# Weighted sums over keys in three 64-column passes, in a hybrid SSD and attention layer

## The chip, the cores and the metric

The kernel runs on one NeuronCore of a Trainium2 chip. The metric is the device time of one execution in microseconds (us). Five engines work side by side, each on its own queue in order: PE (TensorE, the matrix multiplier; PEld is its weight loader), DVE (VectorE), ACT (ScalarE), POOL (GpSimd) and SP (SyncE, which here issues the DMAs). PE writes its results to PSUM, of which the kernel uses 8 banks of 128 partitions by 512 columns; DVE and ACT read them back.

## The reference, cut to what matters

One decoder layer over 512 positions of width 1024: an RMS norm, then two mixers side by side (a Mamba-2 SSD with 16 heads of 64 and an attention with 16 heads of 64), an output projection, and a squared-ReLU MLP. All is float32. What the change touches is one step in each mixer, where a matrix of weights over keys multiplies the values of one head:

```python
# SSD, per head: y = (C B^T * decay, lower triangle) @ (dt * x), and then the skip
y = ssd_chunked_scan(xs, dt, a, bm, cm) + d_skip.astype(jnp.float32)[:, None] * xs
# attention, per head: softmax weights (three dilated windows joined) @ v
o = jnp.einsum('brhiqk,brhikd->brhiqd', pr, vb.astype(jnp.float32)) / denom
```

Both are, for one head, a 512 x 512 lower triangular matrix of weights W (queries by keys) times a 512 x 64 matrix of values t.

## The kernel before

**Split operands.** The kernel multiplies operands of type fp32r. It splits each float32 operand in two parts, hi (a cast to fp32r) and lo (what the cast left over, also cast), and adds up products of parts in PSUM. A dense product (`mm3`, lines 151 to 154) takes three passes: hi by hi, hi by lo, lo by hi.

**The weighted sum.** `weighted_sum` (lines 635 to 641) is called by `ssd_sum` and `att_sum`, once for each of 32 heads. W lies transposed, keys on partitions, in four blocks of 128 keys; block j holds only the queries that may see it: 512, 384, 256 and 128 of them (`BLK`), 1280 columns in all (`OFF` are their starts). There is a tile for its hi part (`wk_H`, `Wh` in the function) and one for its lo part (`wk_L`, `Wl`). The values of a pair of heads lie in one tile (`xd` for SSD, `vhl` for attention): for each block of keys and each head 64 columns of hi beside 64 columns of lo. The function loads these 128 columns as weights, so that rows 0 to 63 of the result hold (value hi) x W and rows 64 to 127 hold (value lo) x W, and passes W's hi part and W's lo part through them: 8 matmuls. All four products of parts are made. The two halves of the PSUM bank must then be added.

**Reading the result.** In SSD `ssd_add` (lines 707 to 713) does it on DVE: line 711 adds the skip to rows 0 to 63, line 713 adds rows 64 to 127. In attention `att_copy` (line 936) copies rows 0 to 63 on ACT to `ya`, and `att_add` (line 941) adds rows 64 to 127 on DVE. The bank is free after that last addition.

**What sets the order.** From 157 us to 507 us of the span the order on every engine is made by a planner, `place_units` (lines 1051 to 1119). The program states several hundred units of work, each with engine, cost in ns, what it needs and makes, what it takes from and gives back to pools of buffers, and a due time; a unit marked "ACT/DVE" or "POOL/DVE" has two costs and goes where it would end first. Again and again the planner takes, among the units that are ready, the one that can start first by these costs (with a slack, within which the earlier due time wins), and appends it to its engine's queue. In this stretch PE does five kinds of work: dense products of the input projection (`hh`, `hl`; 32 jobs of 24 matmuls) and of half of the output projection (`yh`, `yl`), which are due late and so fill gaps; score products (lines 866 and 869); transposes by a product with the identity (lines 649, 838, 912); sums over rows and spreads of scales (1218, 1219, 799, 732); and the 32 weighted sums (line 640). DVE does for each SSD head the product with the decay (line 693) and the lo part (701), for each attention head the row maxima (879), most normalisations (902) and the lo part (925), and beside them the dot products of the conditioning vector (280). The chip's engines then follow the queues in order, and wait at a semaphore where something that a unit needs is late.

Behind 507 us come the other half of the output projection and the MLP, which the change leaves as they were.

Of the kernel before, what the change touches and what calls it, by code (L numbers as in the profile page):

```python
# [17 lines left out]
P = 128  # L18
# [8 lines left out]
BLK = [512, 384, 256, 128]  # L27
# [17 lines left out]
def tile_hybrid_layer(ctx, tc, xT, vec, c_row, ada_e, ada_r, w_a, w_dt, w_x, w_z, w_v, w_qk,  # L45
# [588 lines left out]

    def weighted_sum(p, t, e, Wh, Wl):

        W = Wh, Wl
        for n, (j, i) in enumerate(((0, 0), (0, 1), (1, 0), (1, 1), (2, 0), (3, 0), (2, 1), (3, 1))):
            m = (2 * j + e) * P
            nc.tensor.matmul(p[:, j * P:], lhsT=t[:, m:m + P], rhs=W[i][:, OFF[j]:OFF[j] + BLK[j]],  # L640
                             start=n == 0, stop=n == 7)

    S = {}

# [58 lines left out]
    def ssd_sum(h, p):  # L703
        sums_o[h] = p
        weighted_sum(p, xdt[h // 2], h % 2, S.pop(("H", h)), S.pop(("L", h)))

    def ssd_add(h):
        c, e = h // 2, h % 2
        p = sums_o.pop(h)
        r = slice(e * 64, e * 64 + 64)  # L710
        nc.vector.scalar_tensor_tensor(xs[c][r], xs[c][r], vecs[r, V_DS + c:V_DS + c + 1], p[:64],
                                       op0=OP.mult, op1=OP.add)
        nc.vector.tensor_add(xs[c][r], xs[c][r], p[64:])

    def gate_mul(g):

# [215 lines left out]
    def att_copy(h):  # L932
        if h % 2 == 0:
            yatt.append(zp.tile([P, T], F32, tag="z8", name="ya"))
        r = slice(h % 2 * 64, h % 2 * 64 + 64)
        nc.scalar.copy(yatt[h // 2][r], S["ao", h][:64])

    def att_add(h):
        r = slice(h % 2 * 64, h % 2 * 64 + 64)
        y = yatt[h // 2]  # L940
        nc.vector.tensor_add(y[r], y[r], S.pop(("ao", h))[64:])

    def ssq_sq(pair):
        if pair:
# [101 lines left out]
    def unit(eng, cost, fn, needs=(), makes=None, take=(), give=(), due=0.0, lands=0):  # L1046
        units.append((eng, cost, fn, tuple(needs), makes, tuple(take), tuple(give), due, lands))
# [76 lines left out]
    def xbank(key):  # L1124
        return bank(2 + rooms["x", key])
# [139 lines left out]
    for h in range(16):  # L1265
        c = h // 2
        unit("SP", 350, lambda h=h: dec_load(h), [], ("A", h), [("A", ("s", h))], due=h - 2, lands=4500)
        unit("POOL", 1450, lambda h=h: dec_trim(h), [("A", h)], ("trim", h), due=h - 0.5)
        unit("ACT", 2150, lambda h=h: dec_exp(h), [("trim", h)] + ([] if h else [("z", 1)]), ("exp", h), due=h)
        needs = [("exp", h)] + ([("cb3", n) for n in range(3)] if h >= 12 else [("cb0", h // 4)])  # L1270
        unit("DVE", 1850, lambda h=h: wt_mul(h), needs, ("mul", h),
             give=[("cb", h // 4)] if h % 4 == 3 else [], due=h + 0.3)
        unit("ACT", 1270, lambda h=h: wt_hi(h), [("mul", h)], ("hi", h), [("H", ("s", h))], due=h + 0.4)
        unit("DVE", 2050, lambda h=h: wt_lo(h), [("hi", h)], ("lo", h), [("L", ("s", h))],
             [("A", ("s", h))], due=h + 0.5)
        unit("PE", 1180, lambda h=h: ssd_sum(h, xbank(("so", h))), [("hi", h), ("lo", h), ("xdt", c)],
             ("so", h), [("x", ("so", h))],
             [("H", ("s", h)), ("L", ("s", h))] + ([("xd", c)] if h % 2 else []), due=h + 0.6)
        unit("DVE", 1460, lambda h=h: ssd_add(h), [("so", h)], ("sy", h), give=[("x", ("so", h))],
             due=h + 0.8)  # L1280


# [94 lines left out]
    for a in range(16):  # L1377
        p, e = a // 2, a % 2
        t = AT + a
        A = ("A", ("a", a))  # L1380
        for n in range(3):
            k = ("sp", a, n)
            unit("PE", (440, 480, 260)[n], lambda a=a, n=n: att_scores(a, n, xbank(("sp", a, n))),
                 [("sk", p), ("sq", p), ("ql", p, e)] + ([("sp", a, n - 1)] if n else []), k, [("x", k)],
                 ([("ql%d" % e, p)] + ([("st", p)] if e else [])) if n == 2 else [], due=t)
            unit("DVE", (690, 850, 420)[n], lambda a=a, n=n: att_max(a, n),
                 [k, "mask"] + ([("mx", a, n - 1)] if n else []), ("mx", a, n), [A] if n == 0 else [],
                 [("x", k)], due=t + 0.1)
        unit("DVE", 180, lambda a=a: att_neg(a), [("mx", a, 2)], ("neg", a), due=t + 0.2)
        unit("ACT", 3050, lambda a=a: soft(*S["soft", a]), [("neg", a)], ("soft", a), due=t + 0.2)  # L1390
        unit("DVE", 170, lambda a=a: att_inv(a), [("soft", a)], ("inv", a), due=t + 0.4)
        for i in range(4):
            unit("ACT/DVE", ((370, 320), (480, 430), (600, 540), (730, 650))[i],
                 lambda eng, a=a, i=i: att_norm(a, i, eng), [("inv", a)], ("norm", a, i), due=t + 0.4)
        for n in range(3):
            k = ("fl", a, n)
            unit("PE", (460, 460, 230)[n], lambda a=a, n=n: att_flip(a, n, xbank(("fl", a, n))),
                 [("norm", a, i) for i in ((0, 1, 2, 3), (1, 2, 3), (2, 3))[n]], k, [("x", k)],
                 [A] if n == 2 else [], due=t + 0.5)
            unit("ACT", (590, 590, 375)[n], lambda a=a, n=n: att_hi(a, n),  # L1400
                 [k] + ([("ah", a, n - 1)] if n else []), ("ah", a, n), [] if n else [("H", ("a", a))],
                 due=t + 0.6)
            unit("DVE", (690, 690, 430)[n], lambda a=a, n=n: att_lo(a, n),
                 [("ah", a, n)] + ([("al", a, n - 1)] if n else []), ("al", a, n),
                 [] if n else [("L", ("a", a))], [("x", k)], due=t + 0.7)
        k = ("ao", a)
        unit("PE", 1180, lambda a=a: att_sum(a, xbank(("ao", a))), [("al", a, n) for n in range(3)] + [("vl", p, e)], k,
             [("x", k)], [("H", ("a", a)), ("L", ("a", a))] + ([("vhl", p)] if e else []), due=t + 0.8)
        unit("ACT", 590, lambda a=a: att_copy(a), [k], ("yc", a), [] if e else [("z8", ("y", p))],
             due=t + 0.9)  # L1410
        unit("DVE", 690, lambda a=a: att_add(a), [("yc", a)], ("ya", a), give=[("x", k)], due=t + 1)
        if e:
            k = ("ss", p)
            if p:
                unit("ACT", 630, lambda p=p: ssq_sq(p), [("ya", a), ("ya", a - 1)], k, [("f2", k)],
                     due=t + 1)
                unit("POOL", 1400, lambda p=p: ssq_add(p), [k, ("ssq", p - 1)], ("ssq", p),
                     give=[("f2", k)], due=t + 1)
            else:
                unit("ACT", 630, lambda p=p: ssq_sq(p), [("ya", a), ("ya", a - 1)], ("ssq", 0), due=t + 1)  # L1420
# [214 lines left out]
```

## Time and profile before

| | |
|---|---|
| time, median of 3 executions | 914.64 us (911.78 to 915.18) |
| the profiled execution's own time | 912.53 us, of which the span of its instructions is 910.8 us |
| granted TensorE clock, mean | 0.983 of full speed |
| busy share of the span | PE 93%, DVE 69%, ACT 48%, POOL 30% |
| stretch made by the planner | 157 to 507 us, 350 us |
| in it: PE, DVE, ACT, POOL busy | 323.67, 308.85, 242.29, 210.35 us |

The views of a profile are these. The page gives busy times, the span in 40 slices, and the chain of work that ended last, followed back from the last instruction. The view of groups puts instructions of one line, engine and form in one row: busy time, mean duration, and the engine's idle time just before them. The view of windows gives each engine's busy time in a stretch. The view of waits says who waited for whom. The timeline lists instructions in order of start. Matmuls are pipelined and their ends are modelled: in a row of matmuls each starts before the one ahead has ended, and the time that each costs is the distance from start to start.

### The profile page before, as it was taken

To read this page: it belongs to the slowest core of one execution; us is meant where nothing else is said; L and a number is where in the kernel's file an instruction comes from. 1 tells how busy PE (TensorE), PEld (TensorE's weight loads), DVE (VectorE), ACT (ScalarE), POOL (GpSimd) and SP (SyncE) were. 2 spreads that over 40 slices of the span, in tenths; PEclk is the share of its full clock that TensorE was granted. 3 is DMA by queue.
4 is the path that set the end of the run, shared out by engine and by line. 5 is a ranking of instruction groups with operands and counts; after the bars stand their busy time and mean duration, and the time that the engine had idled before them with its cause. 6 is when DMAs were issued, how large, how long until landed. Compare 5 with 4: busy or idle time off the path is not lost.

```text
span 910.8 us, 11334 instructions
## 1 busy us (share of the span) xinstructions
PE 851.4 (93%) x4112; PEld 709.8 (78%) x4112; DVE 624.2 (69%) x1017; ACT 436.6 (48%) x759; POOL 277.7 (30%) x177
## 2 busy tenths in 40 slices
PE   4988899999898778999899998999999999999998
PEld 4656787878786667788787798988888888888887
DVE  7999976898999889986988678764322234343321
ACT  4225446769664467777866535343212233332110
POOL 3323336486978736556242212000000000000000
PEclk9999999999999999999999999999999999999999
DMA  9743345443644734433442323452232222333320
GB/s 330 255 161 121 109 130 194 156 157 128 212 136 137 230 99 141 129 102 116 140 139 70 116 59 127 152 195 93 96 111 94 93 93 94 106 101 104 119 100 24
DMA packets 43111, 120.01 MB, mean 132 GB/s; under 512 B 5264, under 2 KB 5792, under 8 KB 43056
## 3 DMA queue, kind: packets, MB, share of 16 engines
q1 hardware_dynamic: 43056, 119.29, 40.0%
q8 instruction: 32, 0.52, 0.2%
q14 instruction: 23, 0.19, 0.1%
HBM read 108.70 MB, written 2.18 MB: 122 GB/s over the span
## 4 chain that ended last, share of the span: by engine, by line
PE 65%; DVE 25%; DMA 3%; ACT 3%; issue 3%; POOL 0%; SPq 0%; DVEq 0%; POOLq 0%
PE ps L152 19%; PE ps L153 19%; PE ps L154 19%; PE ps L640 3%; DVE wa L280 3%; DVE ada L280 3%; DMA ada<-in_ada_r_dram 2%; DVE wk_L L701 2%; DVE wk_A L902 1%; DVE wk_A L879 1%; DVE wk_A L693 1%; DVE f L585 1%; ACT wk_A L85 1%; PE ps L912 1%; DVE raw L804 1%
## 5 line engine op out<-in xcount | busy, mean ns | idle before, releaser
L114 ACT CAST whi<-wraw 128x1024 fp32r<-128x1024 f32 (+1 forms) x84 | 86.4, 1031 | 247.7 <-PE ps L153 225.1
L117 DVE TENSOR_TENSOR wlo<-wraw,whi 128x1024 fp32r<-128x1024 f32 x66 | 80.7, 1224 | 133.7 <-ACT whi L114 132.2
L152 PE MATMUL ps<-hh,whi 128*128 128x512 f32 (+1 forms) x390 | 158.2, 409 | 9.3 <-DVE f L585 5.1
L153 PE MATMUL ps<-hl,whi 128*128 128x512 f32 (+1 forms) x390 | 156.6, 401 | 2.2 <-DVE hl L127 2.2
L154 PE MATMUL ps<-hh,wlo 128*128 128x512 f32 (+1 forms) x390 | 156.0, 400 | 0.0
L1145 POOL TENSOR_TENSOR wlo<-wraw,whi 128x1024 fp32r<-128x1024 f32 x40 | 108.6, 2720 | 73.5 <-ACT whi L1141 66.0
L153 PE MATMUL ps<-ul,whi 128*128 128x512 f32 (+1 forms) x272 | 102.4, 377 | 0.0
L154 PE MATMUL ps<-uh,wlo 128*128 128x512 f32 (+1 forms) x272 | 102.4, 377 | 0.0
L152 PE MATMUL ps<-uh,whi 128*128 128x512 f32 (+1 forms) x272 | 102.4, 377 | 0.0
L152 PEld LDWEIGHTS ps<-hh,whi 128*128 128x128 f32 x390 | 76.0, 196 | 26.7 <-issue 5.7
L153 PEld LDWEIGHTS ps<-hl,whi 128*128 128x128 f32 x390 | 76.8, 197 | 18.1 <-DVE hl L127 3.7
L154 PEld LDWEIGHTS ps<-hh,wlo 128*128 128x128 f32 x390 | 76.7, 197 | 16.4
L152 PE MATMUL ps<-h2h,whi 128*128 128x512 f32 x224 | 87.1, 389 | 0.0
L153 PE MATMUL ps<-h2l,whi 128*128 128x512 f32 x224 | 87.1, 389 | 0.0
L154 PE MATMUL ps<-h2h,wlo 128*128 128x512 f32 x224 | 87.1, 389 | 0.0
L280 DVE CUSTOM_DVE_ANT_0 ada<-ada 128x512 f32<-128x512 f32 x64 | 67.7, 1068 | 20.8 <-DMA ada<-in_ada_r_dram 20.6
L117 POOL TENSOR_TENSOR wlo<-wraw,whi 128x1024 fp32r<-128x1024 f32 (+1 forms) x18 | 41.2, 2288 | 93.9 <-ACT whi L114 93.9
L152 PEld LDWEIGHTS ps<-uh,whi 128*128 128x128 f32 x272 | 51.2, 188 | 9.5
L153 PEld LDWEIGHTS ps<-ul,whi 128*128 128x128 f32 x272 | 51.2, 188 | 9.4
L154 PEld LDWEIGHTS ps<-uh,wlo 128*128 128x128 f32 x272 | 51.2, 188 | 9.3
L1551 DVE SCALAR_TENSOR_TENSOR x<-ps,modc,x 128x512 f32<-128x512 f32 (+1 forms) x17 | 12.2, 719 | 60.6 <-PE ps L154 60.6
L153 PEld LDWEIGHTS ps<-h2l,whi 128*128 128x128 f32 x224 | 42.1, 188 | 8.8
(291 smaller groups left out, 1790.2 us busy)
## 6 DMA issues: line engine op xcount, KB each, us to landing
wraw<-in_w_f_dram SPq DMA_DIRECT2D x60, 512.0 KB, 3.3
ada<-in_ada_r_dram SPq DMA_DIRECT2D x64, 256.0 KB, 3.4
wk_A<-arow_d SPq DMA_DIRECT2D x16, 640.0 KB, 4.4
wa<-in_ada_e_dram SPq DMA_DIRECT2D x16, 512.0 KB, 6.8
wraw<-in_w_qk_dram SPq DMA_DIRECT2D x16, 512.0 KB, 3.8
wraw<-in_w_o_dram SPq DMA_DIRECT2D x16, 512.0 KB, 3.3
wraw<-in_w_x_dram SPq DMA_DIRECT2D x10, 512.0 KB, 3.3
wraw<-in_w_z_dram SPq DMA_DIRECT2D x8, 512.0 KB, 4.4
```

The lines of the kernel that those rows point to most:

```text
L85: return nc.scalar.activation(out_, in_, func, **kw)
L114: a = nc.scalar.copy(hi, src)
L117: return a, (leng or nc.vector).tensor_tensor(lo, src, f(hi), op=OP.subtract)
L152: pinned(nc.tensor.matmul(dst, lhsT=lh, rhs=rh, start=start, stop=False), pin)
L153: nc.tensor.matmul(dst, lhsT=lh, rhs=rl, start=False, stop=False)
L154: nc.tensor.matmul(dst, lhsT=ll, rhs=rh, start=False, stop=stop)
L280: return nc.vector.tensor_tensor_reduce(out=w, in0=w, in1=c, scale=1.0, scalar=0.0, op0=OP.mult, op1=OP.add, accum_out=dst)
L585: nc.vector.scalar_tensor_tensor(acc[:, d:], p[:, :T - d], w(i), acc[:, d:], op0=OP.mult, op1=OP.add)
L640: nc.tensor.matmul(p[:, j * P:], lhsT=t[:, m:m + P], rhs=W[i][:, OFF[j]:OFF[j] + BLK[j]], start=n == 0, stop=n == 7)
L701: nc.vector.tensor_tensor(S["L", h], dec[h], f(S["H", h]), op=OP.subtract)
L1145: nc.gpsimd.tensor_tensor(lo, S.pop(("wraw", j)), f(hi), op=OP.subtract)
L1551: nc.vector.scalar_tensor_tensor(x1[n][:, t], p[:, t], modc[:, 3, n:n + 1], x1[n][:, t], op0=OP.mult, op1=OP.add)
```

## The change

`weighted_sum` makes three passes over each block of W with 64 columns of values as weights: value hi by W hi, value lo by W hi, value hi by W lo. All three go to rows 0 to 63 of the bank. The product of the two lo parts is no longer made, as in the dense products. Line 713 and `att_add` go, `att_copy` hands the bank back, and the costs that the planner is told follow: 1750 ns in place of 1180 for the sum, 750 in place of 1460 for `ssd_add`.

```diff
     def weighted_sum(p, t, e, Wh, Wl):
 
-        W = Wh, Wl
-        for n, (j, i) in enumerate(((0, 0), (0, 1), (1, 0), (1, 1), (2, 0), (3, 0), (2, 1), (3, 1))):
-            m = (2 * j + e) * P
-            nc.tensor.matmul(p[:, j * P:], lhsT=t[:, m:m + P], rhs=W[i][:, OFF[j]:OFF[j] + BLK[j]],
-                             start=n == 0, stop=n == 7)
+        p, t = p[:64], parts(t)
+        for j in range(4):
+            for i, (s, W) in enumerate(((0, Wh), (1, Wh), (0, Wl))):
+                nc.tensor.matmul(p[:, j * P:], lhsT=t[:, j, e, s, :], rhs=W[:, OFF[j]:OFF[j] + BLK[j]],
+                                 start=j == 0 and i == 0, stop=j == 3 and i == 2)
...
-        nc.vector.tensor_add(xs[c][r], xs[c][r], p[64:])
...
-        nc.scalar.copy(yatt[h // 2][r], S["ao", h][:64])
-
-    def att_add(h):
-        r = slice(h % 2 * 64, h % 2 * 64 + 64)
-        y = yatt[h // 2]
-        nc.vector.tensor_add(y[r], y[r], S.pop(("ao", h))[64:])
+        nc.scalar.copy(yatt[h // 2][r], S.pop(("ao", h))[:64])
...
-        unit("PE", 1180, lambda h=h: ssd_sum(h, xbank(("so", h))), [("hi", h), ("lo", h), ("xdt", c)],
+        unit("PE", 1750, lambda h=h: ssd_sum(h, xbank(("so", h))), [("hi", h), ("lo", h), ("xdt", c)],
...
-        unit("DVE", 1460, lambda h=h: ssd_add(h), [("so", h)], ("sy", h), give=[("x", ("so", h))],
+        unit("DVE", 750, lambda h=h: ssd_add(h), [("so", h)], ("sy", h), give=[("x", ("so", h))],
...
-        unit("PE", 1180, lambda a=a: att_sum(a, xbank(("ao", a))), [("al", a, n) for n in range(3)] + [("vl", p, e)], k,
+        unit("PE", 1750, lambda a=a: att_sum(a, xbank(("ao", a))), [("al", a, n) for n in range(3)] + [("vl", p, e)], k,
...
-        unit("ACT", 590, lambda a=a: att_copy(a), [k], ("yc", a), [] if e else [("z8", ("y", p))],
-             due=t + 0.9)
-        unit("DVE", 690, lambda a=a: att_add(a), [("yc", a)], ("ya", a), give=[("x", k)], due=t + 1)
+        unit("ACT", 590, lambda a=a: att_copy(a), [k], ("ya", a), [] if e else [("z8", ("y", p))],
+             [("x", k)], due=t + 0.9)
```

Since the planner's costs change, its order changes over the whole stretch. Over the program PE has 384 matmuls of weighted sums in place of 256; DVE has 32 additions fewer, but 11 casts of line 759 (`sq_hi`, the hi part of squares, an "ACT/DVE" unit) in place of 5, and 51 normalisations in place of 52; ACT has 9 of those casts in place of 15 and 13 normalisations in place of 12. POOL and SP have as many instructions as before.

On PE, around the end of the fourth and the start of the fifth SSD head's sum, there stood before (the number behind a tile's name tells its buffers apart):

```order
L640 MATMUL ps_1611<-wk_H_1567,xd_1404 128x128
L640 MATMUL ps_1611<-wk_L_1584,xd_1404 128x256
L640 MATMUL ps_1611<-wk_L_1584,xd_1404 128x128
L152 MATMUL ps_1575<-hh_457,whi_1439 128x512
L153 MATMUL ps_1575<-hl_458,whi_1439 128x512
...
L154 MATMUL ps_1575<-hh_498,wlo_1440 128x512
L640 MATMUL ps_1629<-wk_H_1593,xd_1546 128x512
L640 MATMUL ps_1629<-wk_L_1607,xd_1546 128x512
```

and now:

```order
L640 MATMUL ps_1593<-wk_H_1556,xd_1408 64x128 x2
L640 MATMUL ps_1593<-wk_L_1567,xd_1408 64x128
L640 MATMUL ps_1614<-wk_H_1575,xd_1502 64x512 x2
L640 MATMUL ps_1614<-wk_L_1589,xd_1502 64x512
L640 MATMUL ps_1614<-wk_H_1575,xd_1502 64x384 x2
L640 MATMUL ps_1614<-wk_L_1589,xd_1502 64x384
L640 MATMUL ps_1614<-wk_H_1575,xd_1502 64x256 x2
```

Each sum has twelve matmuls with 64 columns of weights in place of eight with 128, and the six dense matmuls that stood between these two sums have moved. Between the first and the last of the 16 SSD sums stand 330 dense matmuls now, 390 before.

On DVE, in the SSD part, the additions go out of the queue (an excerpt of the difference, - before and + after; `wk_L` is the lo part of W, `xd` the values):

```order
 L701 TENSOR_TENSOR wk_L<-wk_A,wk_H 128x1280
 L711 SCALAR_TENSOR_TENSOR xs<-xs,vecs,ps 64x512
-L713 TENSOR_TENSOR xs<-xs,ps 64x512
 L667 TENSOR_TENSOR xd<-f_1390,xd 128x8x64
 L701 TENSOR_TENSOR wk_L<-wk_A,wk_H 128x1280
```

What follows in the queue stands one instruction nearer to its front.

On DVE, at the normalisation (902, now 901) of the second attention head, there stood before:

```order
L894 RECIPROCAL stat<-stat 128x4
L902 TENSOR_SCALAR wk_A<-wk_A,stat 128x128
L902 TENSOR_SCALAR wk_A<-wk_A,stat 128x256
L902 TENSOR_SCALAR wk_A<-wk_A,stat 128x384
L902 TENSOR_SCALAR wk_A<-wk_A,stat 128x512
```

and now:

```order
L893 RECIPROCAL stat<-stat 128x4
L901 TENSOR_SCALAR wk_A<-wk_A,stat 128x128
L924 TENSOR_TENSOR wk_L<-ps,wk_H 128x512
L901 TENSOR_SCALAR wk_A<-wk_A,stat 128x256
...
L901 TENSOR_SCALAR wk_A<-wk_A,stat 128x384
L758 CAST sh<-f_2810 128x512
L924 TENSOR_TENSOR wk_L<-ps,wk_H 128x256
```

A cast of line 759 (now 758) that the planner has given to DVE stands ahead of the last lo part (925, now 924) for which the first head's weighted sum waits.

## The prediction

> **What bounds the kernel now.** First the page: busy times of the engines, and the chain of work that ended last by engine.
>
> ```profile
> PE 851.4 (93%) x4112; PEld 709.8 (78%) x4112; DVE 624.2 (69%) x1017; ACT 436.6 (48%) x759; POOL 277.7 (30%) x177
> ...
> PE 65%; DVE 25%; DMA 3%; ACT 3%; issue 3%; POOL 0%; SPq 0%; DVEq 0%; POOLq 0%
> ```
>
> PE bounds the whole, but averages hide the stage. So next the windows, of which the stretch from 157 to 507 us holds all that the change touches (columns: length, then busy time and instructions per engine, granted clock, DMA share, GB/s).
>
> ```profile
> core 0: us, PE busy (x) PEld busy (x) DVE busy (x) ACT busy (x) POOL busy (x), PEclk, DMA share, GB/s
> ...
> 200.00:250.00 50.00, 47.30 (x217) 39.22 (x216) 45.51 (x40) 38.45 (x62) 40.67 (x26) 0.94 0.48 173
> 250.00:300.00 50.00, 46.63 (x225) 38.02 (x224) 48.63 (x51) 27.27 (x44) 40.79 (x24) 1.00 0.42 138
> 300.00:350.00 50.00, 40.34 (x186) 32.59 (x185) 43.01 (x100) 31.09 (x69) 25.51 (x16) 0.93 0.61 166
> ...
> 157.00:507.00 350.00, 323.67 (x1590) 267.30 (x1589) 308.85 (x520) 242.29 (x478) 210.35 (x123) 0.98 0.44 139
> 507.00:911.00 404.00, 397.51 (x1973) 338.51 (x1971) 181.48 (x266) 127.58 (x178) 12.45 (x9) 1.00 0.32 105
> ```
>
> Two engines are nearly full here: PE idles for 350 - 323.67 = 26.3 us, DVE for 41.2 us. Behind 507 us PE is full and nothing changes. The waits of PE in the stretch say whom it waits for, the longest first:
>
> ```profile
> PE ps L1219 <- POOL sl L763: 5.3, 4, 2.7
> PE ps L799 <- DVE wk_L L925: 4.9, 1, 4.9
> PE ps L869 <- DVE wk_L L925: 3.4, 3, 1.7
> PE ps L640 <- DVE wk_L L701: 3.4, 3, 2.1
> PE ps L869 <- DVE stat L879: 2.5, 2, 2.2
> ```
>
> Of these 19.5 us, 14.2 are owed to DVE. So PE sets the pace and stops now and then for DVE. The chain of waits in the stretch, by line (shares of 350 us) and with the pieces that the change deletes:
>
> ```profile
> by line: PE ps L152 9.3%; PE ps L153 8.9%; PE ps L154 8.8%; PE ps L640 7.8%; DVE ada L280 5.6%; issue 4.8%; DVE wk_L L701 4.4%; DVE wk_A L902 3.8%; DVE wk_A L879 3.8%; DVE wk_A L693 3.6%; DMA ada<-in_ada_r_dram 3.4%; ACT wk_A L85 3.1%; PE p
> ...
> 283.02 0.69 DVE xs L713
> ...
> 299.26 0.69 DVE xs L713
> 341.29 0.70 DVE ya L941
> ...
> 503.58 0.69 DVE ya L941
> ```
>
> The weighted sums, line 640, are on the chain for 7.8% of 350 = 27.3 us. The deleted additions are on it with ten pieces, three of L713 and seven of L941, of which these are the first and last: 6.1 us in all, eight of them whole at 0.69 us.
>
> **The change part by part.** *A third pass on PE.* The timeline of one sum now, and the dense and transposing work on either side:
>
> ```profile
> 170.66 0.39 PE L154 MATMUL ps<-hh,wlo 128*128 128x512 f32 x1
> 170.88 0.39 PE L640 MATMUL ps<-wk_H,xd 128*128 128x512 f32 x1
> 171.11 0.39 PE L640 MATMUL ps<-wk_L,xd 128*128 128x512 f32 x1
> 171.34 0.33 PE L640 MATMUL ps<-wk_H,xd 128*128 128x384 f32 x1
> 171.51 0.34 PE L640 MATMUL ps<-wk_L,xd 128*128 128x384 f32 x1
> 171.68 0.34 PE L640 MATMUL ps<-wk_H,xd 128*128 128x256 f32 x2
> 171.86 0.40 PE L640 MATMUL ps<-wk_L,xd 128*128 128x256 f32 x2
> 172.09 0.62 PE L649 MATMUL ps<-ident,xs 128*128 128x128 f32 x4
> 172.47 0.48 PE L152 MATMUL ps<-hh,whi 128*128 128x512 f32 x1
> ```
>
> From start to start a block of 512 columns costs 0.23 us, one of 384 0.17, and 256 with 128 together 0.18: a pass is 0.58 us and the eight matmuls take 172.09 - 170.88 = 1.21 us. What the trace lacks is a pass with 64 columns of weights. The nearest row has 48, standing between matmuls with 128:
>
> ```profile
> 61.64 0.39 PE L152 MATMUL ps<-hh,whi 128*128 128x512 f32 x1
> 61.87 0.40 PE L160 MATMUL ps<-hl,wdt 128*48 128x512 f32 x1
> 62.11 0.53 PE L153 MATMUL ps<-hl,whi 128*128 128x512 f32 x1
> ...
> 61.69 0.12 PEld L160 LDWEIGHTS ps<-hl,wdt 128*48 128x48 f32 x1
> 61.87 0.19 PEld L153 LDWEIGHTS ps<-hl,whi 128*128 128x128 f32 x1
> ```
>
> It costs 0.23 us going in and 0.24 coming out, as a matmul with 128 columns does; so neither half the width makes a pass shorter nor does the change of width stop PE. Loading 48 columns takes 0.12 us and 128 take 0.19, so four loads more per sum, all narrower, stay behind the moving data, except perhaps at the three matmuls of 128 columns at a sum's end. There a pass of 128 columns costs between 0.06 us (what is left of 0.18 when 256 columns take half of 0.23) and 0.095 (the four transposes above, with 128 columns each, take 172.47 - 172.09 = 0.38 us), so the loss is 0 to 0.1 us a sum. I take 0.575 us a sum: 32 x 0.575 = 18.4 us more work on PE, with 18 and 21.6 as bounds.
>
> *The additions on DVE.* The groups that go, the copy that now ends an attention head, and the cast that wanders (the last row is of the view of one line: shortest, median and longest in ns):
>
> ```profile
> L713 DVE TENSOR_TENSOR xs<-xs,ps 64x512 f32<-64x512 f32 x16 | 11.1, 691 | 0.6
> L941 DVE TENSOR_TENSOR ya<-ya,ps 64x512 f32<-64x512 f32 x16 | 11.0, 690 | 4.0 <-ACT ya L936 3.6
> L936 ACT COPY ya<-ps 64x512 f32<-64x512 f32 x16 | 9.3, 579 | 10.9 <-PE ps L640 10.4
> L759 ACT CAST sh<-f 128x512 fp32r<-128x512 f32 x15 | 9.3, 622 | 3.1 <-PE ps L1218 1.9 <-DVE f L728 1.1
> ...
> L759 DVE CAST sh<-f x5: 412/717/2632, 206.4 to 335.4; 128x512 fp32r<-128x512 f32 x5
> ```
>
> DVE loses 11.1 + 11.0 = 22.1 us. But the planner sees a freer DVE and sends it six casts of line 759 more: at their median of 0.72 us 4.3 us (2.5 at the shortest, 15.8 at the longest). So DVE is relieved by some 18 us, not 22. ACT loses six casts of 0.62 us, 3.7 us, which costs nothing either way: it is busy for 242.29 of the 350 us. The PSUM bank of an attention head comes free after the copy, 0.7 us earlier; a wait of PE for L941 is not among the five longest above, so I give that nothing.
>
> *Sum along the chain.* The sums on the chain grow by 0.575 / 1.21, which is 27.3 x 0.475 = +13.0 us. The additions on it give back 6.1 us. Of the casts I take the share that the additions had on the chain (6.1 of 22.1, 28%): +1.2 us; bounds 0 and 4.3. Together +8.1 us. With the order unchanged this is a floor, for the other PE work is lengthened too; a new order can fill some of it in again, and I let the two cancel. Against the profiled execution's own 912.53 us that gives 920.6; the median is 914.64, 2.1 us above that execution, so the forecast is 914.6 + 8 = 922.6, rounded to **922 us**, 0.8% slower. Its own range is 918 to 928.
>
> **The rivals.** *PE alone decides.* Sums keep their stops: what DVE saves isn't on PE's path, since the stops are owed to single late instructions (one stop of 4.9 us at L799), not to DVE's load. The order speaks for it: two sums now stand back to back where six dense matmuls covered the second's wait for `wk_L`. Then all 18.4 us show: 933 us (928 to 937). Against it: 14.2 us of the waits above end on DVE.
>
> *DVE decides, and the time falls.* From 250 to 300 us DVE is busy for 48.63 of 50 us, and five of the twelve lines that lead the chain are DVE's. If each SSD head is paced by DVE, 16 additions of 0.691 us shorten the SSD part by up to 11.1 us; the dense work left over moves behind it (60 matmuls have moved out already), and PE's 18.4 us go into its 26.3 us of idle time. By the windows that lets the stretch shrink by no more than 26.3 - 18.4 = 7.9 us, with PE never idle: 906.7 us. Since a matmul's modelled end outlasts its pace by 0.39 - 0.23 = 0.16 us, each stop is a little longer than the idle time shows, and the full 11.1 us, 903.5, stays possible; so 902 to 909.5. It decides once PE's stops fall to under 8 us. Against it: PE would have to run all but without a stop, which it does only behind 507 us, where one kind of work is left.
>
> In a sentence apart: the Trainium skill, "Perfetto Trace Analysis", section "Identifying the Most-Contended Engine", holds busy matmul time for a bad measure of the room that PE has and would look at the weight loads; these are busy for 267.30 of 350 us, by which PE had 82.7 us of room and this rival the better odds. The stretch behind 507 us, where PE stands still for next to nothing, has loads busy for 338.51 of 404 us, 84%; so 76% is not much room, and I leave the odds.
>
> *Both cancel.* The stops that DVE ends shrink by what the third pass costs on the path: 8.1 us out of 14.2. 914.6 us (910 to 918), and the change does nothing that can be measured.
>
> *Each change of width drains PE.* If a matmul with 64 columns had to wait until the one ahead has left the array, each of 64 changes would cost the difference of a matmul's length to its pace, 0.39 - 0.23 = 0.16 us: 10 us on top of 922, or 932. The row with 48 columns speaks against it, at 0.23 and 0.24 us. Such a rule is in the Trainium skill, "TensorEngine Tiling (Array Packing)", section "Key Properties": a change of tiling mode, not merely of tile, drains TensorE. The trace shows no such stop at 48 columns, though whether 64 count as another mode no run here shows.
>
> **How the numbers follow.** A difference of 0.5%, about 4.6 us, is what a measurement of this kernel can tell from no change: below 910 is faster, above 919.2 slower. Chances: the forecast 0.42, PE alone 0.12, the drain 0.03, both cancel 0.26, DVE decides 0.17. Of the forecast's range the lower end, 918 to 919.2, is within 0.5%; I count 0.04 of its 0.42 there. So slower 0.38 + 0.12 + 0.03 = 0.53, within 0.26 + 0.04 = 0.30, faster 0.17. The range goes from 906, within the case of the faster time, to 932, within that of PE alone; it leaves out about one in ten at either end.
>
> **What would show it.** In the profile after: twelve matmuls of a sum in 1.75 to 1.85 us, and L640 at some 57 us from start to start over 32 heads where it took 39; the stretch up to the last sum longer by 5 to 10 us, and unchanged behind it; PE busy for more of it; DVE's busy time in it lower by 15 to 20 us and DVE idle more; PE's waits for DVE shorter, but by less than 10 us. I am wrong if the stretch is shorter: then PE's waits have fallen below 10 us, and DVE was the pacemaker. I am wrong in the other direction if PE's idle time stays at 26 us and the stretch grows by 18. If a sum takes over 2 us, the loads or the widths cost what I priced at nothing.

## The result, and the profile after

The changed kernel takes 924.38 us (median of four, 924.09 to 924.7) beside 914.01 us (911.78 to 915.18) for the kernel before: a ratio of 1.0117, with a 95% interval of 1.009 to 1.0145. 1.17% of 914 us are 10.7 us (the medians differ by 10.4), where 8 were forecast. The profiled execution took 924.09 us, of which the span is 922.4. The page of the changed kernel begins with busy times, and its part on the chain gives shares by engine:

```profile
PE 865.6 (94%) x4240; PEld 712.6 (77%) x4240; DVE 607.1 (66%) x990; ACT 432.9 (47%) x754; POOL 273.4 (30%) x177
...
PE 64%; DVE 23%; ACT 5%; DMA 4%; issue 4%; SPq 0%; POOL 0%; DVEq 0%; ACTq 0%; POOLq 0%
```

The windows, cut where the last SSD sum starts (287 us) and where the planner's stretch ends (519 us); columns as before:

```profile
157.00:287.00 130.00, 120.80 (x596) 93.98 (x595) 115.56 (x101) 91.60 (x144) 94.22 (x60) 0.99 0.46 156
287.00:519.00 232.00, 217.49 (x1120) 176.43 (x1119) 178.91 (x394) 147.32 (x330) 111.39 (x64) 0.98 0.41 122
157.00:519.00 362.00, 338.29 (x1713) 270.41 (x1712) 294.46 (x494) 238.93 (x474) 205.60 (x124) 0.98 0.42 135
519.00:922.00 403.00, 396.83 (x1969) 338.03 (x1967) 180.68 (x265) 126.81 (x176) 12.46 (x9) 1.00 0.32 105
```

The kernel before, cut in the same way:

```profile
157.00:295.00 138.00, 129.65 (x601) 106.30 (x600) 126.54 (x116) 96.27 (x150) 105.99 (x63) 0.98 0.45 154
295.00:507.00 212.00, 194.02 (x991) 160.99 (x991) 182.31 (x405) 146.02 (x328) 104.35 (x61) 0.98 0.44 129
```

The stretch went from 350 to 362 us; behind it the time is as it was (403 and 404 us). Within it the SSD part became 8 us shorter and the rest 20 us longer: dense products moved out of the first into the second. PE is busy for 14.6 us more (338.29 against 323.67) and stands idle for only 2.6 us less (23.7 against 26.3). What it stands for has changed, as the view of PE's waits in the stretch shows (its six longest rows: total, times, longest):

```profile
PE ps L640 <- DVE wk_L L701: 6.5, 7, 1.5
PE ps L868 <- DMA st<-qh: 5.1, 1, 5.1
PE ps L153 <- DVE yl L993: 3.8, 3, 1.8
PE ps L911 <- DVE stat L878: 2.1, 2, 1.4
PE ps L911 <- DVE wk_L L924: 1.8, 2, 1.6
PE ps L798 <- DVE rhl L117: 1.6, 1, 1.6
```

Gone are the 4.9 us at L799 and most of the 5.3 us for `sl`; new are stops inside the SSD sums (6.5 us in seven, before 3.4 in three), one of 5.1 us for the copies of the queries, and three for the split of the output projection's input. Inside one sum without a stop (the timeline of PE):

```profile
169.16 0.63 PE L640 MATMUL ps<-wk_H,xd 128*64 128x512 f32 x2
169.63 0.39 PE L640 MATMUL ps<-wk_L,xd 128*64 128x512 f32 x1
169.85 0.51 PE L640 MATMUL ps<-wk_H,xd 128*64 128x384 f32 x2
...
170.72 0.28 PE L640 MATMUL ps<-wk_H,xd 128*64 128x128 f32 x2
170.83 0.23 PE L640 MATMUL ps<-wk_L,xd 128*64 128x128 f32 x1
170.89 0.62 PE L649 MATMUL ps<-ident,xs 128*128 128x128 f32 x4
```

170.89 - 169.16 = 1.73 us, 0.52 more than before: 16.6 us over 32 sums.

### The profile page after: what moved, and what is told of

It is laid out like the page before. It is cut to its first block, busy times and chain, and to the rows that moved or that the text cites. A ratio compares the mean times of both kernels' runs of the same rounds, so it can differ in the third digit from the quotient of the medians.

```text
span 922.4 us, 11577 instructions
## 1 busy us (share of the span) xinstructions
PE 865.6 (94%) x4240; PEld 712.6 (77%) x4240; DVE 607.1 (66%) x990; ACT 432.9 (47%) x754; POOL 273.4 (30%) x177
## 4 chain that ended last, share of the span: by engine, by line
PE 64%; DVE 23%; ACT 5%; DMA 4%; issue 4%; SPq 0%; POOL 0%; DVEq 0%; ACTq 0%; POOLq 0%
PE ps L152 19%; PE ps L154 19%; PE ps L153 19%; PE ps L640 3%; DVE wa L280 3%; DVE wk_L L701 2%; DMA ada<-in_ada_r_dram 2%; DVE ada L280 2%; DVE wk_A L693 2%; ACT wk_A L85 2%; DVE f L585 1%; PE ps L911 1%; PE ps L868 1%; PE ps L865 1%; DVE yl L993 1%
## 5 line engine op out<-in xcount | busy, mean ns | idle before, releaser
L153 PE MATMUL ps<-hl,whi 128*128 128x512 f32 (+1 forms) x390 | 154.6, 396 | 2.2 <-DVE hl L127 2.2
L154 PE MATMUL ps<-hh,wlo 128*128 128x512 f32 (+1 forms) x390 | 153.7, 394 | 0.0
L1139 POOL TENSOR_TENSOR wlo<-wraw,whi 128x1024 fp32r<-128x1024 f32 x40 | 106.2, 2656 | 65.9 <-ACT whi L1135 56.7
L280 DVE CUSTOM_DVE_ANT_0 ada<-ada 128x512 f32<-128x512 f32 x64 | 60.9, 959 | 27.4 <-DMA ada<-in_ada_r_dram 27.2
L1135 ACT CAST whi<-wraw 128x1024 fp32r<-128x1024 f32 x40 | 42.2, 1055 | 21.0 <-PE ps L153 14.7
```

The source lines that it names most:

```text
L153: nc.tensor.matmul(dst, lhsT=lh, rhs=rl, start=False, stop=False)
L154: nc.tensor.matmul(dst, lhsT=ll, rhs=rh, start=False, stop=stop)
L280: return nc.vector.tensor_tensor_reduce(out=w, in0=w, in1=c, scale=1.0, scalar=0.0, op0=OP.mult, op1=OP.add, accum_out=dst)
L1135: nc.scalar.copy(S["w", j][0], S["wraw", j])
L1139: nc.gpsimd.tensor_tensor(lo, S.pop(("wraw", j)), f(hi), op=OP.subtract)
```

## The experiments

Each ratio is to the kernel before, measured beside it, with its 95% interval. It can differ a little from the quotient of the two medians (most for the casts on ACT, where the medians give 1.0089 and the record 1.0118), and differences in us are worked out from the ratio. The theory on trial is that of the prediction, the chain: sums on the path grow, deleted additions on it are given back, the order adds nothing. Its rivals: PE alone, DVE decides, and, once the first runs were in, the new order itself.

**The third pass alone, in the order of before.** The additions stay, and the third pass repeats the product of W's hi part:

```diff
-        for n, (j, i) in enumerate(((0, 0), (0, 1), (1, 0), (1, 1), (2, 0), (3, 0), (2, 1), (3, 1))):
+        for n, (j, i) in enumerate(((0, 0), (0, 1), (0, 0), (1, 0), (1, 1), (1, 0), (2, 0), (3, 0), (2, 1), (3, 1), (2, 0), (3, 0))):
...
-                             start=n == 0, stop=n == 7)
+                             start=n == 0, stop=n == 11)
```

> The order of before on every engine, the additions kept, and each weighted sum with a third pass of 128 columns of weights (value hi and lo by W hi once more, so the sums hold that product twice): the third pass alone. Base 914.0 us, the median of before. Theory of the chain: the sums stand on the chain for 27.3 us and grow by 0.475 of that, +13.0, as a floor: 927 us (926 to 930). PE alone decides: all of 32 x 0.575 = +18.4 shows: 932 us. DVE decides: the pass goes into PE's idle time: 914 to 919 us.

Measured: 921.77 us, ratio 1.0115 [1.0082, 1.0147], 10.5 us. The chain's 13.0 is just inside the interval, though the time is below the 926 to 930 foreseen. A sum took 1.85 us here (170.87 to 172.73 us), 0.64 more than before, so PE had 20.5 us more work, of which half shows; PE alone is out.

**The additions alone taken away, in the order of before.** Two passes of 128 columns stay:

```diff
-        nc.vector.tensor_add(xs[c][r], xs[c][r], p[64:])
...
-        nc.vector.tensor_add(y[r], y[r], S.pop(("ao", h))[64:])
+        S.pop(("ao", h))
```

> The order of before on every engine with the 32 additions of the upper half taken out of DVE's queue, two passes of 128 columns as before (the products with the lo part of the values are left out of the result): the relief of DVE alone. Theory of the chain: the additions stand on it for 6.1 us: 908 us (906 to 910). PE alone decides: 913 to 914 us, as before. DVE decides: at least the 11.1 us of the SSD part: 903 us or less.

Measured: 906.85 us, ratio 0.9947 [0.9925, 0.9968], -4.8 us. This is as the chain had it (6.1 us, inside the interval). Of 22.1 us taken off DVE a fifth shows; DVE doesn't set the pace.

**The whole change in the order of before.** The planner is told the costs of the kernel before, and a unit that does nothing stands where `att_add` stood:

```diff
-        unit("PE", 1750, lambda h=h: ssd_sum(h, xbank(("so", h))), ...
+        unit("PE", 1180, lambda h=h: ssd_sum(h, xbank(("so", h))), ...
-        unit("DVE", 750, lambda h=h: ssd_add(h), ...
+        unit("DVE", 1460, lambda h=h: ssd_add(h), ...
-        unit("PE", 1750, lambda a=a: att_sum(a, xbank(("ao", a))), ...
+        unit("PE", 1180, lambda a=a: att_sum(a, xbank(("ao", a))), ...
-             [("x", k)], due=t + 0.9)
+             due=t + 0.9)
+        unit("DVE", 690, lambda a=a: att_add(a), [("yc", a)], ("ya", a), give=[("x", k)], due=t + 1)
```

> The change itself, three passes of 64 columns and no additions, but with the planner told the costs and units of before, so that every engine keeps the order of before: the change without the new order. Theory of the chain: +13.0 - 6.1 = +6.9: 921 us (919 to 923); the changed kernel, at 924.4, then paid some 3 us for its new order, where I had taken the new order to pay for what the floor leaves out. PE alone decides: 932 us. DVE decides: 903 to 909 us.

Measured: 916.04 us, ratio 1.003 [1.0007, 1.0052], 2.7 us, below the chain's 919 to 923. This is the run that divides the result: of the 1.17%, 0.30 belong to the work and 0.87 (8 us) to the order. The windows and the longest waits of PE in this run:

```profile
157.00:300.00 143.00, 137.43 (x676) 109.23 (x675) 110.59 (x104) 98.19 (x153) 102.52 (x64) 0.99 0.47 157
300.00:511.00 211.00, 199.58 (x1057) 163.17 (x1055) 170.65 (x385) 145.73 (x329) 103.33 (x61) 0.98 0.42 125
157.00:511.00 354.00, 337.00 (x1729) 272.40 (x1728) 281.23 (x489) 243.93 (x482) 205.85 (x124) 0.99 0.44 138
```

```profile
PE ps L798 <- DVE wk_L L924: 5.0, 1, 5.0
PE ps L1216 <- POOL sl L762: 4.7, 3, 3.2
PE ps L868 <- DVE stat L878: 2.9, 2, 2.2
```

PE is busy for 337.0 us, nearly the 338.29 of the changed kernel, but idle for 17.0 us, not 23.7. In the order of before, idle time of PE takes up 9.3 of the 13.3 us that its busy time grew (26.3 - 17.0, 337.0 - 323.67); in the new order 2.6 of 14.6. DVE is busy for 13 us more in the new order than here (294.46 against 281.23), with nearly the same instructions (six casts more, one normalisation less): many last longer in their new places.

**The new order alone.** The changed kernel with the two passes of 128 columns of before, and no additions:

```diff
-        p, t = p[:64], parts(t)
-        for j in range(4):
-            for i, (s, W) in enumerate(((0, Wh), (1, Wh), (0, Wl))):
...
+        W = Wh, Wl
+        for n, (j, i) in enumerate(((0, 0), (0, 1), (1, 0), (1, 1), (2, 0), (3, 0), (2, 1), (3, 1))):
```

> The changed kernel with its order on every engine, but two passes of 128 columns per sum in place of three of 64 (no additions either, so the products with the lo part of the values are left out): what the third pass costs in the new order. Base 924.4 us, the changed kernel. Theory of the chain: about as much as in the old order, 13 us: 911 us (909 to 914). PE alone decides: 18.4 us: 906 us. DVE decides: 919 us or more.

Measured: 917.4 us, ratio 1.0058 [1.0035, 1.0081]. Beside the run without additions in the order of before (0.9947), the order alone costs 1.1%: with other work the same step as above. The windows of the two runs, first without additions in the order of before:

```profile
157.00:503.00 346.00, 321.60 (x1586) 267.57 (x1585) 280.74 (x489) 242.14 (x480) 210.23 (x124) 0.98 0.44 142
```

and in the new order:

```profile
157.00:510.00 353.00, 323.49 (x1581) 266.53 (x1580) 293.74 (x494) 238.05 (x473) 204.90 (x123) 0.98 0.43 138
```

Of 7 us, 5.1 are idle time of PE (29.5 against 24.4), and DVE is again busy for 13 us more. The third pass, added to this, costs 0.6% (1.0117 against 1.0058), some 5 us of 16.6, where the chain had 13 and PE alone 18.4.

**Which of the told costs makes the order dear.** The change with the longer sum told, and `ssd_add` and `att_add` told as before:

```diff
-        unit("DVE", 750, lambda h=h: ssd_add(h), ...
+        unit("DVE", 1460, lambda h=h: ssd_add(h), ...
-             [("x", k)], due=t + 0.9)
+             due=t + 0.9)
+        unit("DVE", 690, lambda a=a: att_add(a), [("yc", a)], ("ya", a), give=[("x", k)], due=t + 1)
```

> The change, with the planner told the sum's longer cost (1750) but still the additions on DVE as units that issue nothing (1460 and 690): half of the new figures. The old order with the same work took 1.003 of before, the new order 1.0117; the difference, some 8 us, is the order's. If the longer sum makes the order worse (the planner holds PE for fuller and moves dense products out of the SSD part): 1.010 or more, 922 us on a base of 913. If the freer DVE makes it (casts move to DVE, 6 stand there here, 11 in the changed kernel): 1.003, 916 us. If any order but the old one costs: 1.007 or more in this run and in the next.

Measured: 919.48 us, ratio 1.0065 [1.0042, 1.0088]. And the other way about, the freer DVE told and the sums told as before:

```diff
-        unit("PE", 1750, lambda h=h: ssd_sum(h, xbank(("so", h))), ...
+        unit("PE", 1180, lambda h=h: ssd_sum(h, xbank(("so", h))), ...
-        unit("PE", 1750, lambda a=a: att_sum(a, xbank(("ao", a))), ...
+        unit("PE", 1180, lambda a=a: att_sum(a, xbank(("ao", a))), ...
```

> The change, with the planner told that the additions are gone (750, and no unit for attention) but the old cost of the sum (1180): the other half of the new figures. 10 casts of line 759 stand on DVE. If the longer sum makes the order worse: 1.003, 916 us. If the freer DVE makes it: 1.010 or more, 922 us. If any order but the old one costs: 1.007 or more here and in the run before.

Measured: 934.25 us, ratio 1.0225 [1.0201, 1.0249]. The instructions' work is nearly the same in four kernels (the casts and normalisations that may go to either of two engines move a little), and the time differs by 2%: neither told 1.003, the longer sum 1.0065, both 1.0117, the freer DVE alone 1.0225. With the sum told rightly, telling that DVE is freer costs 0.5%; with it told wrongly, 2%. Telling the longer sum costs 0.35% where DVE is told as before, and saves 1.1% where it is told to be freer. So neither new figure is dear by itself: 1.0065 is less than the 1.010 that was to speak for the longer sum, and its interval leaves out the 1.003 that was to speak for the freer DVE. That any order but the old one costs fits both runs (1.007 lies in the first one's interval) and is not ruled out: all three new orders are dearer. One new wait stands out in the last run, PE's for a dot product of the conditioning vector:

```profile
PE ps L868 <- DVE adac L280: 7.5, 1, 7.5
```

Its granted clock was lower too, 0.974 over the whole span against 0.983, and PE is busy for longer:

```profile
157.00:531.00 374.00, 345.85 (x1722) 276.00 (x1721) 293.38 (x496) 241.06 (x475) 201.41 (x121) 0.96 0.41 131
```

Of the 20 us that this stretch is longer than in the order of before, 8.9 are busy time of PE (345.85 against 337.00) and 11.1 idle time (28.1 against 17.0); so a part of the time isn't the order's waits.

**Each half of the change, in the order of before.** Three passes and no addition for the SSD heads alone:

```diff
-        weighted_sum(p, xdt[h // 2], h % 2, S.pop(("H", h)), S.pop(("L", h)))
+        weighted_sum3(p, xdt[h // 2], h % 2, S.pop(("H", h)), S.pop(("L", h)))
...
-        nc.vector.tensor_add(xs[c][r], xs[c][r], p[64:])
```

> The order of before on every engine; three passes of 64 columns and no addition in the 16 SSD sums, attention as before. If SSD is where DVE sets the pace (48.63 of 50 us busy from 250 to 300 us): 11.1 us off DVE against 9.2 us on PE, 0.995 or less, 909 us. If the gain and the loss lie alike in both parts: half of the old order's 1.003, 914 to 915 us. If PE alone decides: 1.010, 922 us.

Measured: 913.77 us, ratio 1.0009 [0.9989, 1.003]. For the attention heads alone:

```diff
-        weighted_sum(p, vhl[h // 2], h % 2, S.pop(("H", h)), S.pop(("L", h)))
+        weighted_sum3(p, vhl[h // 2], h % 2, S.pop(("H", h)), S.pop(("L", h)))
...
-        nc.vector.tensor_add(y[r], y[r], S.pop(("ao", h))[64:])
+        S.pop(("ao", h))
```

> The order of before on every engine; three passes and no addition in the 16 attention sums, SSD as before. SSD alone took 1.0009 of before (0.9989 to 1.003), both together 1.003. If the parts add up: 1.002, 915 us. If the relief of DVE in one part pays only with the other changed too: 1.004 or more here. Theory of the chain: of its 6.1 us of additions 4.7 are attention's, and of the sums' 27.3 us most lie behind 295 us (8.5% of 207 us, 17.6 us, growing by 8.4): +3.7 us, 1.004.

Measured: 913.8 us, ratio 1.0009 [0.999, 1.0028]. Neither half can be told from no change; the chain's 1.004 for the attention half lies outside the interval. DVE decides would have given the SSD half a gain, since DVE is fullest there; none is seen.

**The changed kernel once more, beside the two runs with half of the told costs and on their chip.**

> The changed kernel again, on the same chip as the three runs beside it: 1.0117 (1.009 to 1.0145) as measured first; if the order's share was a matter of that chip it would be at 1.003 to 1.006.

Measured: 924.82 us, ratio 1.0118 [1.0093, 1.0143].

**The casts.** In the new order eleven casts of line 758 (759 before) run on DVE. Here they are issued on ACT, everything else where it was:

```diff
-        (eng.copy if eng is nc.scalar else eng.tensor_copy)(S["sh", g], S["sq", g])
+        nc.scalar.copy(S["sh", g], S["sq", g])
```

> The changed kernel with the order on every engine kept, but the 11 casts of line 758 that the planner gave to DVE issued by ACT, at the place in its queue where they stand in the program: whether the wandering casts are what makes the new order dear. Base 1.0117 of before. If the casts stop DVE (two of them took 2.2 and 2.6 us beside a POOL instruction, nine some 0.42): 1.007 or less, 919 us. If the new order costs by what PE waits for elsewhere (the lo parts of the SSD weights behind sums that stand back to back, the copies of the queries, the output projection's operands): 1.010 or more, 923 us. The forecast held the casts for 1.2 us of its 8.1.

Measured: 921.64 us, ratio 1.0118 [1.0087, 1.0149]. The 1.007 or less of casts that stop DVE is out: they aren't the main part of what the order costs. The 1.2 us that the forecast had for them is less than this run can tell from nothing.

**The stops inside the sums.** The changed kernel, with W's lo part used last in each sum:

```diff
-        for j in range(4):
-            for i, (s, W) in enumerate(((0, Wh), (1, Wh), (0, Wl))):
+        for i, (s, W) in enumerate(((0, Wh), (1, Wh), (0, Wl))):
+            for j in range(4):
```

> The changed kernel in its own order, but with the matmuls of every weighted sum in another sequence: first the eight that read the hi part of W (wk_H), then the four that read the lo part (wk_L). Nothing of the computation is left out, and no other instruction moves. The lo part is first needed 1.15 us into the sum instead of 0.45 us, 0.7 us later. Theory A: the new order is dear because PE now stops inside the SSD sums for the lo part (seven stops of 0.9 to 1.7 us, 6.5 us of waits in all, since sums stand back to back). Then each stop shrinks by 0.7 us, about 5 us in all: 919 to 920.5 us, ratio 1.006 to 1.008 against the kernel before. Theory B: the new order is dear because of what stands where in the attention part (dense matmuls that are left over there and a late copy of the queries), and a stop saved in the SSD sums is given back at the next wait: 923 to 926 us, ratio 1.010 to 1.014, as the changed kernel has it.

Measured: 923.32 us, ratio 1.0108 [1.0085, 1.0131]. Theory A's 1.006 to 1.008 is out. Each sum has 0.7 us more before it needs the lo part, and yet PE's stops for it did not shrink; the wait row of this run, and the row of the lo part among DVE's groups in the SSD part (busy, mean ns, idle time before):

```profile
PE ps L640 <- DVE wk_L L701: 7.3, 8, 2.1
```

```profile
L701 DVE TENSOR_TENSOR wk_L<-wk_A,wk_H 128x1280 fp32r<-128x1280 f32 x16 | 38.1, 2390 | 0.1
```

Directly ahead of the 16 instructions of L701 DVE is idle for 0.1 us in all: the lo part comes when DVE's queue reaches it, whenever PE needs it. PE merely came to the next stop sooner, and waited there. The stops were moved and not taken away, so the run doesn't show what they cost; nor does it show theory B's reason, the attention part.

**The same idea in the kernel before.**

```diff
-        for n, (j, i) in enumerate(((0, 0), (0, 1), (1, 0), (1, 1), (2, 0), (3, 0), (2, 1), (3, 1))):
+        for n, (j, i) in enumerate(((0, 0), (1, 0), (2, 0), (3, 0), (0, 1), (1, 1), (2, 1), (3, 1))):
```

> The kernel before in its own order, but with the four matmuls of every weighted sum that read the hi part of W first, and then the four that read the lo part; in the kernel before the second matmul already reads the lo part. Nothing of the computation is left out. The lo part is first needed 0.58 us into the sum instead of 0.23 us, 0.35 us later. If PE's stops inside the sums are on the path that sets the end (four in the trace of the kernel before: 2.3, 0.8, 0.8 and 0.7 us), each shrinks by 0.35 us, at most 1.4 us: 912 to 913 us, ratio 0.998 to 0.999. If they are given back at the next wait: 914 us, ratio 1.000. Either is within what this measurement can tell; a ratio below 0.996 would say that stops before the lo part cost more than the trace shows.

Measured: 914.03 us beside 913.66, ratio 1.0009 [0.9991, 1.0027]: no change that can be told.

Only the run without additions is faster than both kernels. It leaves out the value's lo part altogether, so it is no version of the same sum.

## Why the prediction came out as it did

The time, 924.4 against 922, lies in the forecast's own range of 918 to 928. Its working does not hold in the same measure: two errors of opposite sign stand in it, so that the time came out so near is in part luck.

**The step that failed: "a new order can fill some of it in again, and I let the two cancel".** The order was set at nothing. It costs 0.87%, 8 us (the change in the new order and in that of before), and 1.1% with two passes. It filled nothing in; it opened PE's idle time. The lines of the order showed sums back to back and dense matmuls moved out of the SSD part, and the prediction used that only as arguments for rivals, PE alone and DVE decides.

**"With the order unchanged this is a floor" was wrong too.** The order unchanged gives +2.7 us (interval 0.6 to 4.7), not +6.9, which is what the terms without the casts make (13.0 - 6.1). The additions were sized well: -6.1 foreseen, -4.8 measured, inside the interval. The third pass was oversized: with no additions in either kernel it adds 1.003 - 0.9947 = 0.83%, 7.6 us, where 13.0 were taken from the chain. The size of the pass is the smaller part of that: with the measured 0.52 us a sum the chain would have given 27.3 x 0.52 / 1.21 = 11.7. A chain says what lay on the path of one execution. When a piece of it grows, PE's idle time is used up elsewhere (24.4 us without additions, 17.0 with the third pass), and less than the piece's share comes through. The chain of the order-unchanged run shows this:

```profile
by line: PE ps L152 11.0%; PE ps L153 10.7%; PE ps L154 10.6%; PE ps L640 10.5%; issue 4.2%; PE ps L911 3.4%; DVE wk_A L878 3.4%; DMA wk_A<-arow_d 3.2%; DVE wk_L L701 3.1%; DVE wk_A L901 2.8%; POOL wk_A L683 2.6%; DVE qz L820 2.2%; ACT wk_A
```

L640 has 10.5% of 354 = 37.2 us, 9.9 more than before, but DVE's dot products of line 280, 5.6% before, are no longer among the leaders. So the sum by measured terms is 7.6 - 4.8 + 8.0 = 10.8 us, where the prediction had 13.0 - 6.1 + 1.2 + 0. (The three measured terms are differences along one row of runs, so they add up to the measured change by construction.)

**The casts.** +1.2 us was taken for them; moving them to ACT changes nothing that can be measured (1.0118 against 1.0117).

**What the profile was to show.** A sum takes 1.73 us, foreseen 1.75 to 1.85: the third pass costs 0.52 and not 0.575 us. With 128 columns of weights it costs 0.64 (the run with the third pass alone). The likely reason, argued and not shown, is that wide loads hold up the matmuls of 128 moving columns at a sum's end: a load takes 0.188 us with 128 columns and 0.134 with 64, and the last three matmuls follow each other at 0.06 us. So the price of nothing for loads and widths was right, with a small gain that the prediction left out. The stretch is 12 us longer (5 to 10 foreseen) and unchanged behind it, as foreseen. PE's idle time all but stayed at 26 us (23.7), which was half of the sign for being wrong in the other direction; the stretch didn't grow by 18. DVE is idle more (67.5 against 41.2 us). Its busy time in it fell by 14.4 us, just under the 15 to 20 foreseen. Not through the casts: five took 6.4 us before and eleven take 9.2 now, 2.8 more, where 4.3 were allowed. Other instructions of unchanged number took longer or shorter in their new places, the lo part of the queries at line 820 (821 before) most (the groups of DVE in the stretch, before and then after: busy, mean ns):

```profile
L821 DVE TENSOR_TENSOR qz<-raw,qh 64x512 fp32r<-64x512 f32 x12 | 11.7, 972 | 0.9 <-PE ps L866 0.8
```

```profile
L820 DVE TENSOR_TENSOR qz<-raw,qh 64x512 fp32r<-64x512 f32 x12 | 18.7, 1557 | 1.1 <-PE ps L865 0.8 <-ACT vhl L842 0.2
```

PE's waits for DVE were to be shorter, but by less than 10 us. The 14.2 us in the prediction are only the longest rows of before; all rows of PE's waits for DVE in the stretch make 19.4 us before, 17.2 now and 11.6 with the change in the order of before.

**The rivals.** PE alone is out: its 932 us stand against 921.8 for the third pass by itself. DVE decides is out: 22.1 us off DVE bring 4.8. Both cancel comes nearest for the work itself (916.04 against 912.67 with the order unchanged); the order made the rest. The drain did not happen: a matmul of 64 columns behind one of 128 starts 0.22 us after it (168.94 to 169.16) and is followed at 0.235:

```profile
168.94 0.39 PE L154 MATMUL ps<-hh,wlo 128*128 128x512 f32 x1
169.16 0.63 PE L640 MATMUL ps<-wk_H,xd 128*64 128x512 f32 x2
```

**What stays open.** That the new order is dear, and that most of this is idle time of PE, is shown. Which of the told costs makes it so is not: the two act together, and it may be that any order but the old one costs. Which piece of the order does it is not shown either. None of the three new kinds of stop was taken away: those inside the sums were only moved, and those for the query copies (5.1 us) and for `yl` (3.8 us) were not tried. In the runs with the casts on ACT and with the lo part last they stand as they did, and the time with them; but a cause spread over many places would look the same. The dearest order (1.0225) speaks for that: its waits of PE for `yl` and for the lo parts of SSD are 0.3 and 0.2 us, and it waits elsewhere.

## What to carry to other kernels

Where a planner makes the order, a change of work comes with a change of order, and here the second was worth three times the first: measure the change once in the old order, by telling the planner the old costs, and take the order as a term of its own with both signs in the range. A group's share of the chain gave more than its growth cost here; PE's idle time took up some of it first. A stop for an instruction that another engine reaches without a gap wasn't shortened by needing its result later.

## What was not expected of the hardware

An instruction of DVE that starts while one of POOL is under way can last several times as long. The casts on DVE in the changed kernel (shortest, median, longest in ns), and one of them in the timeline beside POOL's subtraction:

```profile
L758 DVE CAST sh<-f x11: 414/420/2636, 199.4 to 424.1; 128x512 fp32r<-128x512 f32 x11
```

```profile
227.41 2.80 POOL L1139 TENSOR_TENSOR wlo<-wraw,whi 128x1024 fp32r<-128x1024 f32 x1 [0.82 <-POOL wk_A L683]
227.86 2.64 DVE L758 CAST sh<-f 128x512 fp32r<-128x512 f32 x1
```

The cast takes 0.42 us by itself; here it begins 0.45 us after POOL's instruction and ends at 230.50, 0.29 us after POOL's end at 230.21. The lo part of W shows the same: 1.49 us at 166.88, and 3.68 us at 171.14, while POOL subtracts twice from 168.26 to 173.47; it ends 1.35 us after that, about its own length. A sum's next matmul waited 1.52 us for this one.

```profile
166.88 1.49 DVE L701 TENSOR_TENSOR wk_L<-wk_A,wk_H 128x1280 fp32r<-128x1280 f32 x1
...
171.14 3.68 DVE L701 TENSOR_TENSOR wk_L<-wk_A,wk_H 128x1280 fp32r<-128x1280 f32 x1
```

```profile
168.26 5.21 POOL L1139 TENSOR_TENSOR wlo<-wraw,whi 128x1024 fp32r<-128x1024 f32 x2 [7.14 <-issue]
```

The Trainium skill, "SBUF — State Buffer", section "SBUF: two separate sides", says that DVE and GpSimd share one pair of ports as an exclusive lock: where a DVE instruction in a two-port mode, or with two inputs in SBUF, meets a GpSimd instruction, the later one waits for the whole of the earlier one. The trace agrees: in both places the DVE instruction ends only behind POOL's. Of the 16 lo parts of SSD weights in the changed kernel ten started while POOL was at work, and all ten end 1.34 to 1.36 us after POOL; the other six took 1.48 to 1.49 us. In the kernel before ten of twelve do the same; two took 1.48 us although a row of POOL began before them, and these rows of POOL are long themselves (one 4.52 us, where the usual is 2.4). So the shortest duration of a DVE instruction is its price without POOL, and a new order changes who meets POOL.

The new stops for `yl` come from this. First the eight instructions of the changed kernel, then those of the change in the order of before:

```profile
L993 DVE SCALAR_TENSOR_TENSOR yl<-xs,vecs,yh x8: 739/740/2851, 441.2 to 448.8; 128x512 fp32r<-128x512 f32 x8
```

```profile
L996 DVE SCALAR_TENSOR_TENSOR yl<-xs,vecs,yh x8: 741/742/989, 435.2 to 440.1; 128x512 fp32r<-128x512 f32 x8
```

Three of the eight took 2.62, 1.78 and 2.85 us in the new order, each beginning behind the start of a POOL instruction, and PE stopped for just these three. The last of them, which begins at 448.80, with POOL and PE:

```profile
448.74 2.36 POOL L1139 TENSOR_TENSOR wlo<-wraw,whi 128x1024 fp32r<-128x1024 f32 x1 [1.08 <-ACT whi L1135]
451.71 0.50 PE L153 MATMUL ps<-yl,whi 128*128 128x512 f32 x1 [1.77 <-DVE yl L993]
```

How much of the order's 8 us is owed to such meetings no run here tells.

A load of 64 columns of weights takes 0.134 us where one of 128 takes 0.188 (rows of the weight loads, changed kernel and the run with the third pass alone):

```profile
L640 PEld LDWEIGHTS ps<-wk_H,xd x128: 133/134/137, 163.3 to 286.7; 128*64 128x64 f32 x128
```

```profile
L640 PEld LDWEIGHTS ps<-wk_H,xd x128: 186/188/192, 163.2 to 296.5; 128*128 128x128 f32 x128
```

Half the columns save 29% of the load. A pass of 512 moving columns takes as long with either (0.235 and 0.23 us).
